# Weights 48 bytes instead of 64 behind the streamed operands, modulo 128, in a two-layer decoder trunk

## The chip, the cores and the metric

The kernel runs on one core of a Trainium2 chip. The metric is the device time of one execution in microseconds (us), the median of several executions.

## The reference

Two layers over 256 tokens of width 1024. Each layer normalizes its input, projects it once into the columns of three token mixers (retention, forgetting attention, RWKV-7) and three gates, merges the mixers' outputs by the gates, projects, and adds a SwiGLU feed-forward block.

```python
for l in range(DEPTH):                       # DEPTH = 2
    h = _rmsnorm(x, mix_norm[l])             # x: (1, 256, 1024)
    proj = (h @ w_in[l]).astype(jnp.float32)
    ret_c, fox_c, rwkv_c, gate_c = jnp.split(proj, splits, axis=-1)
    y_ret = _retention_branch(ret_c, ...)
    y_fox = _fox_branch(fox_c, ...)
    y_rwkv = _rwkv7_branch(rwkv_c, ...)
    gates = jax.nn.sigmoid(gate_c).reshape(B, S, N_BRANCH, D)
    merged = (gates[:, :, 0] * (y_ret @ p_ret[l])
              + gates[:, :, 1] * (y_fox @ p_fox[l])
              + gates[:, :, 2] * (y_rwkv @ p_rwkv[l]))
    x = x + merged @ w_out[l]
    h = _rmsnorm(x, ffn_norm[l])
    g, u = jnp.split(h @ w_gate_up[l], 2, axis=-1)
    x = x + (jax.nn.silu(g) * u) @ w_down[l]
```

Everything is float32.

## The kernel before

**Matrix products in three parts.** Tokens lie along the free axis (256 columns), features on the 128 partitions. Each float32 operand is split into a high part, rounded to the matmul type fp32r, and a low part, the rest. A product of one 128x128 block of weights with 256 tokens is then three matmuls into one accumulator (`mm3`): high weights by high tokens, high weights by low tokens, low weights by high tokens. The weights are the operand that is loaded into the array (LDWEIGHTS, 128 columns), the tokens are streamed past it (MATMUL, 256 columns). Every matmul loads anew, so the PE queue is a strict alternation of loads and matmuls, and a load runs beside the matmul ahead of it. Two groups of products turn the roles round (`gemm_n`, tiles `mqk` and `mv`): the tokens are loaded, and 512, 260 or 256 columns of weights are streamed.

**Where weights come from.** `_piece` takes 1 MB of weights by one DMA into a tile `raw` (three buffers). ACT writes the high part of a piece of up to 1040 columns into `whi`, DVE the low part into `wlo` (pool `spl`, four buffers each), three pieces ahead of their use (`refill`). A piece holds eight 128x128 blocks, so it feeds 24 matmuls.

**Where the streamed tokens lie.** The normalized input is in tiles `xh` and `xl` (pool `xp`), the feed-forward's hidden units in `hi` and `lo` (pool `hp`), the mixers' outputs in `hi` and `lo` of the pool `t2`. A tile's row in a partition is 2048 bytes, two streams of 1024 bytes. Pools lie one behind the other in SBUF, in the order `cp`, `raw`, `spl`, `xp`, and then `big`, `t2`, `sm` for the mixers or `hp`, `ft` for the feed-forward. The allocator puts a tile at a multiple of 32 bytes. Three small tiles that `pad` makes, one at the head of each of `xp`, `big` and `hp`, shift what lies behind them; a buffer of `whi` or `wlo` is 4224 bytes (33 times 128) and one of `raw` 8320 (65 times 128), so all buffers of a pool stand alike modulo 128.

In the built program the streamed tiles of all three pools start at 32 modulo 128, and `whi` and `wlo` at 96. I call the address of the loaded operand less that of the streamed one, modulo 128, their distance. In `mm3` it is 64 throughout (weights less tokens). In `gemm_n` it is tokens less weights: 64 for 512 and 256 columns, and for 260 columns, whose rows are 1040 bytes, it goes 64, 48, 32, 16 over the four blocks of a piece.

The scheduler keeps each engine's instructions in an order that the same code always gives; `PACE` holds the planner's numbers and isn't touched.

Of the kernel before, what the change touches and what calls it, by code (L numbers as in the profile page):

```python
# [9 lines left out]
F32R = mybir.dt.float32r  # L10
# [6 lines left out]
P = 128  # L17
# [143 lines left out]
class Kernel:  # L161
    def __init__(self, ctx, tc, d, depth=DEPTH, debug=None):
        self.tc, self.nc, self.d, self.depth = tc, tc.nc, d, depth
        self.debug = debug or {}
        nc = self.nc
        e = ctx.enter_context
        self.cp = e(tc.tile_pool(name="cp", bufs=1))
        self.raw = e(tc.tile_pool(name="raw", bufs=3))
        self.spl = e(tc.tile_pool(name="spl", bufs=4))
        self.xp = e(tc.tile_pool(name="xp", bufs=4))  # L170
        self.ps = e(tc.tile_pool(name="ps", bufs=4, space=bass.MemoryType.PSUM))
        self.dr = e(tc.tile_pool(name="dr", bufs=1, space=bass.MemoryType.DRAM))
        self.uid, self.pend = 0, None


        zero = self.cp.tile([P, T], mybir.dt.bfloat16, name="zero")
        nc.vector.memset(zero, 0.0)
        pz = self.ps.tile([P, T], F32, tag="sm", bufs=SM, name="pz")
        for _ in range(20):
            self.mmul(pz, zero[:, 0:P], zero, start=True, stop=True)  # L180
        par = [self.cp.tile([P, P_RES], F32, name=f"par{l}") for l in range(depth)]

        self.pad(self.xp, 16)
        self.xt = [self.xtile(f"x0_{j}") for j in range(4)]
        self.jobs, self.raws, self.ready, self.cur = list(self.weights()), [], [], []
        w = [self.raw.tile([P, 2080], F32, tag="raw", name=self.nm("raw")) for _ in range(3)]

        nc.sync.dma_start(w[0][:, 0:1024 + KT], d["x0"])
        self.first = self.halves(w[0][:, 512:1024])
        self.gain = w[0][:, 1024:1024 + KT], self.cp.tile([P, KT], F32, name="gain0")  # L190
        nc.gpsimd.tensor_copy(self.gain[1], self.gain[0])
        nc.sync.dma_start(w[1][:, 0:1536], d["win0"][0, :, 512:2048])
        nc.sync.dma_start(w[2][:, 0:1024], d["win0"][1, :, 0:1024])
        nc.sync.dma_start(self.xt[1], d["xt"][:, 2:4, :])
        nc.sync.dma_start(w[2][:, 1024:2048], d["win0"][1, :, 1024:2048])
        nc.sync.dma_start(self.xt[2], d["xt"][:, 4:6, :])
        self.jobs[0:2] = [(w[0], 2, P, 0), (w[0], 2, P, 2), (w[1], 4, P, 0), (w[1], 8, P, 4), (w[2], 16, P, 0)]
        self.par = par
        self.con = con = self.cp.tile([P, C_RES], F32, name="con")
        self.identb, self.maskb = zero[:, 0:P], zero[:, P:]  # L200
        self.c = {}
        for k, (o, n) in C_OFF.items():
            if k in FETCHED:
                continue
            v = con[:, o:o + n]
            if k in C_SHAPE:
                v = v.rearrange("p (a b) -> p a b", a=C_SHAPE[k][0])
            self.c[k] = v
        cc = self.c["cc"]
        self.cc = lambda i: cc[:, i:i + 1]  # L210
# [87 lines left out]
    def _piece(self):  # L298

        nc = self.nc  # L300
        if not self.raws:
            src, n, width, o = self.jobs.pop(0)
            if hasattr(src, "shape") and src.shape[-1] == n * width:
                raw = self.raw.tile([P, 2080], F32, tag="raw", name=self.nm("raw"))
                nc.sync.dma_start(raw[:, :n * width], src)
            else:
                raw = src
            per = min(8, 1040 // width)
            for s in range(0, n, per):
                self.raws.append((raw, o + s, min(per, n - s), width))  # L310
        raw, s, m, width = self.raws.pop(0)
        r = raw[:, s * width:(s + m) * width]
        hi = self.spl.tile([P, 1056], F32R, tag="whi", name=self.nm("whi"))
        lo = self.spl.tile([P, 1056], F32R, tag="wlo", name=self.nm("wlo"))
        nc.scalar.copy(hi[:, :m * width], r)  # L315
        nc.vector.tensor_tensor(out=lo[:, :m * width], in0=r, in1=hi[:, :m * width].bitcast(F32), op=ALU.subtract)  # L316
        self.ready.append([(hi[:, i * width:(i + 1) * width], lo[:, i * width:(i + 1) * width]) for i in range(m)])
# [1005 lines left out]
```

## Time and profile before

| | |
|---|---|
| median of three runs | 781.5 us (780.92 to 782.41) |
| profiled execution, its own time | 780.94 us |
| its span, first to last instruction | 779.2 us |
| PE busy | 771.7 us, 7000 matmuls |
| DVE busy | 569.0 us |
| ACT busy | 410.6 us |
| granted TensorE clock | 1.00 |

Matmuls overlap in the records, so PE's busy time says only that it never stood still for long. What one matmul costs in the stream is the step from its start to the start of the next, and it is read from start times: a count of instructions in a stretch, divided into the stretch. PEld rows are the weight loads.

### The profile page before, as it was taken

Reading aid. Unit: us, or ns where it says so; the run is one execution under the profiler, and the core shown is the slowest. Engines: PE = TensorE matmul, PEld = TensorE weight load, DVE = VectorE, ACT = ScalarE, POOL = GpSimd, SP = SyncE. Lnnn points to the kernel's source line nnn. Section 1 sums busy time; section 2 is a strip of 40 time slices with the busy share of each in tenths; the row PEclk is TensorE's granted clock in tenths of the full one; section 3 lists DMA queues with packets and bytes.
Section 4 is the critical chain, followed back from the end, with each engine's and each line's share of the span. In section 5 each row is a group of like instructions: output and inputs, shape, how many; then the busy total and the mean of one; then the engine's idle time right before and its main releaser. Section 6 shows DMA issues by size and latency. Waiting matters only on the chain. (4 is left out here: it accounts for less than half of the span.)

```text
span 779.2 us, 16469 instructions
## 1 busy us (share of the span) xinstructions
PE 771.7 (99%) x7000; PEld 754.4 (97%) x7000; DVE 569.0 (73%) x882; ACT 410.6 (53%) x578; POOL 16.7 (2%) x54
## 2 busy tenths in 40 slices
PE   9999999999999999999999999999999999999998
PEld 8899999999999999999998998999999999999998
DVE  7886999688776666655678679987788776666442
ACT  6776555445664445444447855544456554444331
POOL 4000000000000000000020000000000000000000
PEclk9999999999999999999999999999999999999999
DMA  9656445235655555556564453551464556555650
GB/s 340 223 217 188 152 137 206 83 137 216 210 183 188 192 205 180 197 177 209 173 219 169 170 163 126 170 191 62 169 226 173 185 195 214 171 211 171 213 185 28
DMA packets 28235, 140.69 MB, mean 181 GB/s; under 512 B 7648, under 2 KB 9216, under 8 KB 13312
## 3 DMA queue, kind: packets, MB, share of 16 engines
q1 hardware_dynamic: 28160, 139.63, 51.7%
q8 instruction: 55, 0.90, 0.5%
q14 instruction: 20, 0.16, 0.1%
HBM read 137.24 MB, written 1.33 MB: 178 GB/s over the span
## 5 line engine op out<-in xcount | busy, mean ns | idle before, releaser
L315 ACT CAST whi<-raw 128x1024 fp32r<-128x1024 f32 (+3 forms) x258 | 265.1, 1030 | 298.5 <-PE mm L227 215.4
L316 DVE TENSOR_TENSOR wlo<-raw,whi 128x1024 fp32r<-128x1024 f32 (+3 forms) x258 | 308.4, 1199 | 141.1 <-ACT whi L315 140.5
L227 PE MATMUL mm<-xh,whi 128*128 128x256 f32 x1312 | 359.9, 280 | 0.3 <-DVE xh L482 0.2
L227 PE MATMUL mm<-xh,wlo 128*128 128x256 f32 x1312 | 357.7, 279 | 0.0
L227 PE MATMUL mm<-xl,whi 128*128 128x256 f32 x1312 | 357.2, 278 | 0.0
L227 PEld LDWEIGHTS mm<-xh,whi 128*128 128x128 f32 x1312 | 243.5, 188 | 1.1 <-ACT whi L315 0.4
L227 PEld LDWEIGHTS mm<-xh,wlo 128*128 128x128 f32 x1312 | 242.9, 188 | 0.6 <-DVE wlo L316 0.2
L227 PEld LDWEIGHTS mm<-xl,whi 128*128 128x128 f32 x1312 | 243.0, 188 | 0.6 <-DVE xl L491 0.2
L227 PE MATMUL mm<-hi,whi 128*128 128x256 f32 x576 | 160.0, 278 | 0.0
L227 PE MATMUL mm<-hi,wlo 128*128 128x256 f32 x576 | 159.7, 277 | 0.0
L227 PE MATMUL mm<-lo,whi 128*128 128x256 f32 x576 | 159.5, 277 | 0.0
L227 PEld LDWEIGHTS mm<-hi,whi 128*128 128x128 f32 x576 | 108.2, 188 | 0.4
L227 PEld LDWEIGHTS mm<-hi,wlo 128*128 128x128 f32 x576 | 108.2, 188 | 0.3 <-issue 0.3
L227 PEld LDWEIGHTS mm<-lo,whi 128*128 128x128 f32 x576 | 108.1, 188 | 0.1
L699 DVE TENSOR_TENSOR t<-mm,rstd 128x512 f32<-128x512 f32 (+1 forms) x24 | 15.2, 646 | 9.3 <-PE mm L227 8.7
L705 DVE TENSOR_TENSOR h<-t,mm 128x512 f32<-128x512 f32 x22 | 15.1, 687 | 9.4 <-PE mm L227 8.6
L227 PE MATMUL mv<-whi,xh 128*128 128x260 f32 (+1 forms) x64 | 18.7, 292 | 0.0
L227 PE MATMUL mv<-wlo,xh 128*128 128x260 f32 (+1 forms) x64 | 18.2, 285 | 0.0
L648 DVE SCALAR_TENSOR_TENSOR gate<-gate,mm 128x512 f32<-128x512 f32 x24 | 16.1, 679 | 2.8 <-PE mm L227 2.8
L227 PE MATMUL mv<-whi,xl 128*128 128x260 f32 (+1 forms) x64 | 18.1, 283 | 0.0
L640 DVE TENSOR_TENSOR gate<-mm,rstd 128x512 f32<-128x512 f32 x24 | 16.5, 687 | 1.2 <-PE mm L227 0.9
L641 ACT ACTIVATE gate<-gate 128x512 f32<-128x512 f32 x24 | 15.1, 631 | 4.0 <-DVE gate L640 4.0
(252 smaller groups left out, 647.3 us busy)
## 6 DMA issues: line engine op xcount, KB each, us to landing
raw<-in_wg SPq DMA_DIRECT2D x44, 1024.0 KB
raw<-in_wgate SPq DMA_DIRECT2D x24, 1024.0 KB
raw<-in_wd SPq DMA_DIRECT2D x16, 1024.0 KB
raw<-in_win SPq DMA_DIRECT2D x12, 1024.0 KB
raw<-in_wo SPq DMA_DIRECT2D x8, 1024.0 KB
raw<-in_wd SPq DMA_DIRECT2D x8, 768.0 KB
raw<-in_wqk SPq DMA_DIRECT2D x4, 1024.0 KB
raw<-in_pp SPq DMA_DIRECT2D x4, 1024.0 KB
```

The costliest lines, as they stand in the source:

```text
L227: return self.pinned(self.nc.tensor.matmul(*a, **k))
L315: nc.scalar.copy(hi[:, :m * width], r)
L316: nc.vector.tensor_tensor(out=lo[:, :m * width], in0=r, in1=hi[:, :m * width].bitcast(F32), op=ALU.subtract)
L640: nc.vector.tensor_tensor(out=g, in0=ps, in1=self.b2(rstd), op=ALU.mult)
L641: nc.scalar.activation(g, g, AF.Tanh, scale=0.5)
L648: nc.vector.scalar_tensor_tensor(out=g, in0=g, scalar=1.0, in1=ps, op0=ALU.add, op1=ALU.mult)
L699: nc.vector.tensor_tensor(out=t[:, o, :], in0=p, in1=self.bs(rstd, o), op=ALU.mult)
L705: nc.vector.tensor_tensor(out=h, in0=t, in1=pu, op=ALU.mult)
```

## The change

Two edits, no instruction added, removed or moved. The pad tile at the head of `xp` grows from 16 to 20 floats; with the allocator's step of 32 bytes, all that lies behind it moves up by 32 bytes. The tiles `whi` and `wlo` are taken from their fifth element on, 16 bytes further.

```diff
-        self.pad(self.xp, 16)
+        self.pad(self.xp, 20)
...
-        hi = self.spl.tile([P, 1056], F32R, tag="whi", name=self.nm("whi"))
-        lo = self.spl.tile([P, 1056], F32R, tag="wlo", name=self.nm("wlo"))
+        hi = self.spl.tile([P, 1056], F32R, tag="whi", name=self.nm("whi"))[:, 4:]
+        lo = self.spl.tile([P, 1056], F32R, tag="wlo", name=self.nm("wlo"))[:, 4:]
```

| start modulo 128 | before | after |
|---|---|---|
| `whi`, `wlo` | 96 | 112 |
| streamed `xh`, `xl`, `hi`, `lo` | 32 | 64 |
| distance in `mm3` | 64 | 48 |
| distance in `gemm_n`, 512 and 256 columns | 64 | 80 |
| distance in `gemm_n`, 260 columns, block by block | 64, 48, 32, 16 | 80, 64, 48, 32 |
| `con` (identity, masks), `raw` | 32, 96 | 32, 96 |

All other tiles of `xp` and of the pools behind it move by the same 32 bytes and keep their distances to each other. The order of instructions is the same on every engine; one memset of the pad writes four more floats.

## The prediction

> **What bounds the kernel now.** I read the page first, for the engines' shares.
>
> ```profile
> span 779.2 us, 16469 instructions
> PE 771.7 (99%) x7000; PEld 754.4 (97%) x7000; DVE 569.0 (73%) x882; ACT 410.6 (53%) x578; POOL 16.7 (2%) x54
> PEclk9999999999999999999999999999999999999999
> ```
>
> PE is never without work, at full clock. Next the chain of work that ended last, in order of time (start, us, what, count), and what the weight loads waited for (us in total, times, longest):
>
> ```profile
> 555.70 46.26 PE mm L227 x408
> ...
> 602.30 8.53 PE mm L227 x72
> ...
> 611.26 164.60 PE mm L227 x1449
> ...
> PEld mm L227 <- ACT whi L315: 0.4, 1, 0.4
> ...
> PEld mm L227 <- DVE wlo L316: 0.2, 1, 0.2
> ```
>
> The chain is matmuls of line 227 in an unbroken file. Loads waited 0.6 us in all for the split weights, so neither ACT, DVE nor the DMAs set the pace. But the pace isn't uniform: 164.60 / 1449 = 113.6 ns a matmul in one piece, 8.53 / 72 = 118.5 in another of the same instructions. To see why, I asked for stretches, weight loads of line 227 alone (stretch, length, busy and count, clock, DMA share, GB/s); one load of each count reaches over an edge.
>
> ```profile
> 229.03:329.67 100.64, 100.64 (x889) 1.00 0.55 192
> 216.41:223.01 6.60, 6.60 (x57) 1.00 0.42 159
> ...
> 329.67:335.32 5.65, 5.65 (x49) 1.00 0.57 203
> 335.32:389.73 54.41, 54.41 (x482) 1.00 0.56 189
> ```
>
> Two paces: 100.64 / 888 = 113.3 ns, which I call quick, and 6.60 / 56 = 117.9 or 5.65 / 48 = 117.7, which I call slow, at the same clock. There is little between them. Slow stretches begin where the stream was disturbed (small matmuls of the mixers, a new tile) and last some 50 matmuls; quick ones last until the next disturbance. The wide matmuls are these groups, each of them three times over (high by high, high by low, low by high):
>
> ```profile
> L227 PE MATMUL mm<-xh,whi 128*128 128x256 f32 x1312 | 359.9, 280 | 0.3 <-DVE xh L482 0.2
> L227 PE MATMUL mm<-hi,whi 128*128 128x256 f32 x576 | 160.0, 278 | 0.0
> ```
>
> 3 x (1312 + 576) = 5664 of them. Of the 5537 steps from one to the next that the start times give without a break, 4439 are quick (113.3 on average) and 1098 slow (117.9). The slow kind costs 1098 x 4.6 = 5.0 us in all; if all were slow, it would be 4439 x 4.6 = 20.3 us more. These two amounts are the scale of everything below.
>
> **The change, part by part.** The sum is made against the profiled execution, 780.94 us with a span of 779.2; the median of the runs is 781.5, 0.6 above, and I give the forecast against the median.
>
> 1. The pad's memset, 16 to 20 floats on POOL:
>
> ```profile
> L233 POOL MEMSET pad<- x5: 112/113/118, 0.7 to 578.9; 128x16 f32 x3, 128x24 f32 x2
> ```
>
> Forms of 16 and of 24 floats all take 112 to 118 ns, and this one lies at the start, ahead of the first data. Nothing, to within 6 ns.
>
> 2. The splits now write at 16 modulo 32 and read as before. No row has that offset; the nearest is the write of `pj`, whose rows start one float (4 bytes) off the grid, against an aligned write of the same shape:
>
> ```profile
> L640 DVE TENSOR_TENSOR gate<-mm,rstd 128x512 f32<-128x512 f32 x24 | 16.5, 687 | 1.2 <-PE mm L227 0.9
> L747 DVE TENSOR_TENSOR pj<-mm,rstd 128x512 f32<-128x512 f32 x7 | 4.5, 685 | 0.0
> L316 DVE TENSOR_TENSOR wlo<-raw,whi 128x1024 fp32r<-128x1024 f32 x243 | 296.8, 1224 | 134.5 <-ACT whi L315 133.8
> L315 ACT CAST whi<-raw 128x1024 fp32r<-128x1024 f32 x243 | 254.6, 1050 | 285.1 <-PE mm L227 205.7 <-issue 67.7 <-DMA raw<-in_win 4.4
> ```
>
> 685 against 687: no price. The cover, should there be one: a piece feeds 24 matmuls, 24 x 113.3 = 2.7 us, and takes 1.22 us of DVE and 1.05 of ACT; a tenth more on each of 243 pieces is 30 us of a DVE that is idle for 210. Nothing reaches PE.
>
> 3. All tiles behind the pad move by 32 bytes and keep their distances, save against `con`, which stays. That touches the transposes, whose one operand is the identity: for `ptr` from `rav` the distance goes from 32 to 64, from `bk` from 96 to 0. Duration now (ns, min/median/max):
>
> ```profile
> L230 PE MATMUL ptr<-con,rav x16: 272/273/328, 102.7 to 489.0; 128*128 128x128 f32 x16
> ...
> L230 PE MATMUL ptr<-con,bk x16: 272/272/273, 106.9 to 493.3; 128*128 128x128 f32 x16
> ```
>
> The two kinds stand at different distances and take the same. I take nothing; at 1 ns for each of some hundred transposes it is 0.1 us either way.
>
> 4. The distance of the 5664 wide matmuls, 64 to 48: the one term that counts. The trace holds a small trial of it. In `mv` with 260 columns the first block of a piece stands at distance 64 and the second at 48, six matmuls each, in the same stream. Starts of the first block, the second and the third, for the three pieces in which nothing breaks in:
>
> ```profile
> 40.45 0.28 PE L227 MATMUL mv<-whi,xh 128*128 128x260 f32 x1
> ...
> 41.17 0.29 PE L227 MATMUL mv<-whi,xh 128*128 128x260 f32 x1
> ...
> 41.89 0.28 PE L227 MATMUL mv<-whi,xh 128*128 128x260 f32 x1
> ...
> 45.45 0.28 PE L227 MATMUL mv<-whi,xh 128*128 128x260 f32 x1
> ...
> 46.17 0.28 PE L227 MATMUL mv<-whi,xh 128*128 128x260 f32 x1
> ...
> 46.89 0.28 PE L227 MATMUL mv<-whi,xh 128*128 128x260 f32 x1
> ...
> 423.92 0.28 PE L227 MATMUL mv<-whi,xh 128*128 128x260 f32 x1
> ...
> 424.64 0.29 PE L227 MATMUL mv<-whi,xh 128*128 128x260 f32 x1
> ...
> 425.36 0.28 PE L227 MATMUL mv<-whi,xh 128*128 128x260 f32 x1
> ```
>
> At 64: 0.72, 0.72, 0.72 us. At 48: 0.72, 0.72, 0.72. That is 120 ns a matmul both ways, and the second block even streams from an address at 16 modulo 32. The rows resolve 0.01 in 0.72, 1.4% each, about 0.8% over three: 1 ns a matmul, 5.7 us over 5664. So the price is 0, with ends at -5.7 and +5.7 from this trial. What it can't say: 120 is the slow pace (117.9 x 260 / 256 = 119.7); nothing there runs at the quick one, so it is silent on whether the quick pace holds at 48. For that there is only the bound from the stretches, +20.3 if no step stays quick. I take 0, since this is the only row of this very step, and keep -5.7 and the upper end for the range. The reversed matmuls, 512 and 260 columns, go to other distances; at 96 or so of each and 5 ns they can move 1 us at most.
>
> [...]
>
> Sum: 0 + 0 + 0 + 0 on 780.94, so 781.5 at the median.
>
> **The rivals.** *The quick pace is lost, in part or in all (slower).* Load and stream go side by side, and whatever makes 117.9 of 113.3 may need less of a disturbance at 48. For it: addresses do have a say. In 17 places the pace falls from slow to quick inside a run of wide matmuls, at the first block of a new piece; the first and the last of them:
>
> ```profile
> 57.83 0.28 PE L227 MATMUL mm<-xh,whi 128*128 128x256 f32 x1
> ...
> 721.28 0.28 PE L227 MATMUL mm<-hi,whi 128*128 128x256 f32 x1
> ```
>
> In 16 of the 17 that block stands at distance 64 modulo 256, in one at 192, though pieces alternate between the two. After the change these are 48 and 176, and if the way back from slow to quick is gone, slow stretches last. Against it: quick holds for 888 steps through dozens of pieces of both kinds, so it isn't delicate. Price: all slow 801.8; half of the quick ones slow 781.5 + 10.2 = 791.7. It shows from 340 more slow steps on (1.6 us), when the quick share falls from 80% to 74%.
>
> *The slow stretches end sooner or don't arise (faster).* For it: the same 16 of 17. Against it: they begin at disturbances that stay. Price: at most -5.0, and with 512 and 260 columns some -1: 775.5; half of them gone, 779.
>
> *The quick pace itself falls.* Line 230's transposes, each with a load of 128 columns too, follow each other faster:
>
> ```profile
> 106.93 1.04 PE L230 MATMUL ptr<-con,bk 128*128 128x128 f32 x8
> ```
>
> (1.04 - 0.27) / 7 = 110 ns. At 110 the wide ones would save 4439 x 3.3 + 1098 x 7.9 = 23 us: 758. Against it: their streams are half as long, so it needn't be a floor that a distance frees. [...]
>
> That the change doesn't do what it says is ruled out: the built program's addresses stand at 112 and 64. That PE doesn't notice is the forecast.
>
> **How the numbers follow.** No more than 0.2% (1.6 us, about what a measurement of this kernel can tell from no change) either way: 0.36, carried by the equal 0.72 rows. Slow stretches shorter or gone, 775.5 to 779.9: 0.28. The quick pace lower: 0.03. More slow steps, 783.1 to 792: 0.22. Most quick steps lost, 792 to 802: 0.11. The forecast is the likeliest, 781.5. The range 776 to 792 leaves out the third and the last case and the tip of the second, some 0.16. Faster 0.31, same 0.36, slower 0.33. The forecast's own range is 779.9 to 783.1.
>
> **What would show it.** Right: the stretch of gate and up products near 230 to 328 again at 113.3, some 1100 slow steps, the first blocks of `mv` at 0.72. Wrong by the first rival: wide stretches at 117.9 (855 loads in 100.6 us instead of 888), DVE and ACT groups unchanged. Wrong by the second: the piece of 72 after the norm's sum near 602 at 113.3. Casts above 1.05 and 1.22 us would fault step 2, and then loads would wait for `whi` or `wlo`. What would make it wrong above all: that six matmuls at the slow pace say nothing about the quick one.

## The result, and the profile after

The changed kernel takes 809.49 us (809.24 to 809.64), against 781.21 for the kernel before: 1.036 times as long (95% interval 1.035 to 1.038). The profiled execution took 809.64 us. From the page of the changed kernel, the span, PE's row and the granted clock:

```profile
span 807.9 us, 16469 instructions
PE 800.7 (99%) x7000; PEld 783.5 (97%) x7000; DVE 569.7 (71%) x882; ACT 409.4 (51%) x578; POOL 16.7 (2%) x54
PEclk9999999999999999999999999999999999999999
```

The instructions, the clock and the busy time of DVE and ACT are those of before within 0.3%; PE takes longer over the same matmuls, 800.7 us busy against 771.7. Here are the same three pieces of its chain in order of time (start, us, what, count):

```profile
572.24 48.71 PE mm L227 x408
...
621.29 8.61 PE mm L227 x72
...
630.33 174.22 PE mm L227 x1449
```

46.26, 8.53 and 164.60 us have become 48.71, 8.61 and 174.22. The piece of 72, which ran at the slow pace before (118.5 ns), gained 0.08 us; the long one went from 113.6 to 120.2 ns a matmul. So the loss is in what ran at the quick pace. One stretch of the first feed-forward block in both kernels, weight loads of line 227 (stretch, length, busy and count, clock, DMA share, GB/s), before and then after:

```profile
240.00:320.00 80.00, 80.00 (x707) 1.00 0.56 198
```

```profile
240.00:320.00 80.00, 80.00 (x665) 1.00 0.52 185
```

One load of each count reaches over an edge: 80 / 706 = 113.3 ns before, 80 / 664 = 120.5 after. How the new pace is made up shows in the order of time, start by start. At 248.48 a piece of weights begins whose distance is 176 modulo 256 (address of the loaded operand less that of the streamed one), at 251.32 one at 48, at 254.27 one at 176 again; 24 matmuls each.

```profile
248.48 0.28 PE L227 MATMUL mm<-xh,whi 128*128 128x256 f32 x1
...
251.32 0.28 PE L227 MATMUL mm<-xh,whi 128*128 128x256 f32 x1
251.44 0.29 PE L227 MATMUL mm<-xl,whi 128*128 128x256 f32 x1
251.57 0.28 PE L227 MATMUL mm<-xh,wlo 128*128 128x256 f32 x1
251.68 0.29 PE L227 MATMUL mm<-xh,whi 128*128 128x256 f32 x1
251.81 0.28 PE L227 MATMUL mm<-xl,whi 128*128 128x256 f32 x1
...
254.27 0.28 PE L227 MATMUL mm<-xh,whi 128*128 128x256 f32 x1
```

The piece at 176 took 2.84 us, 118.3 ns a matmul; that at 48 took 2.95, 122.9, and in it long and short steps alternate (0.13, 0.11, 0.13: 130 and 117 ns in the records). Not all pieces at 48 are like that: of 88 whole ones 58 go at 123 ns and 30 at 118, so that blocks at 48 average 120.8 and those at 176 118.3. Over the whole run, the 5509 unbroken steps between wide matmuls average 119.5 ns against 114.2 before. 5509 x 5.3 = 29.2 us; the profiled executions differ by 28.7.

What did not change: the splits (DVE and ACT, busy us and mean ns) and the pad's memset, now with a form of 20 floats.

```profile
L316 DVE TENSOR_TENSOR wlo<-raw,whi 128x1024 fp32r<-128x1024 f32 x243 | 296.7, 1224 | 149.9 <-ACT whi L315 149.6
L315 ACT CAST whi<-raw 128x1024 fp32r<-128x1024 f32 x243 | 254.2, 1048 | 315.4 <-PE mm L227 224.9 <-issue 79.8 <-DMA raw<-in_win 4.4
L233 POOL MEMSET pad<- x5: 111/114/119, 0.7 to 596.2; 128x24 f32 x2, 128x16 f32 x2, 128x20 f32 x1
```

### The profile page after: what moved, and what is told of

The parts are those of the page before. It is cut to its first block, busy times and chain, and to the rows that moved or that the text cites. A ratio compares the mean times of both kernels' runs of the same rounds, so it can differ in the third digit from the quotient of the medians.

```text
span 807.9 us, 16469 instructions
## 1 busy us (share of the span) xinstructions
PE 800.7 (99%) x7000; PEld 783.5 (97%) x7000; DVE 569.7 (71%) x882; ACT 409.4 (51%) x578; POOL 16.7 (2%) x54
## 5 line engine op out<-in xcount | busy, mean ns | idle before, releaser
L227 PE MATMUL mm<-xh,whi 128*128 128x256 f32 x1312 | 366.2, 285 | 0.7 <-ACT whi L315 0.5
L227 PE MATMUL mm<-xl,whi 128*128 128x256 f32 x1312 | 363.7, 283 | 0.0
L227 PE MATMUL mm<-xh,wlo 128*128 128x256 f32 x1312 | 363.7, 283 | 0.0
L227 PE MATMUL mm<-hi,whi 128*128 128x256 f32 x576 | 163.2, 283 | 0.0
L227 PE MATMUL mm<-lo,whi 128*128 128x256 f32 x576 | 163.1, 283 | 0.0
L227 PE MATMUL mm<-hi,wlo 128*128 128x256 f32 x576 | 162.6, 282 | 0.0
```

The costliest lines, as they stand in the source:

```text
L227: return self.pinned(self.nc.tensor.matmul(*a, **k))
```

## The experiments

Two theories at the start. Theory D: what counts is the distance between the operand that is loaded and the one that is streamed past. The rivals: it is the place of one operand in itself, the streams' start (A) or the weights' start at 16 modulo 32 (B). All ratios below are against the kernel before, taken with the experiment.

**Both operands moved by 32 bytes, distance 64** (`e1_d64_moved`), **and distance 48 at another place** (`e2_d48_moved`), against the kernel before:

```diff
-        self.pad(self.xp, 16)
+        self.pad(self.xp, 24)      # e2: 32
...                                 # whi and wlo alike
-        hi = self.spl.tile([P, 1056], F32R, tag="whi", ...)
+        hi = self.spl.tile([P, 1056], F32R, tag="whi", ...)[:, 8:]      # e2: 12
```

> Weights and streamed operands both moved by 32 bytes (weights at 0, streams at 64 modulo 128), so the distance is 64 as before. Theory D (the distance between the loaded and the streamed address decides): the pace of before, 113.3 ns with some 118, 781 us within 2. Rival A (where the operands lie in themselves decides, the streams' start at 64 instead of 32 above all): the pace of the changed kernel, 118 to 124 ns, about 809 us.

> Both moved by another 32 bytes against the changed kernel (weights at 16, streams at 96 modulo 128), distance 48 as there. Theory D: the changed kernel again, 809 us within 2, alternating steps of 117 and 130 ns on one half of the pieces. Rival A: something else, since both operands lie elsewhere; about 781 if the streams at 64 were the cause.

Measured: 780.55 us, 0.999 of before (0.998 to 1.000), and 810.45 us, 1.038 (1.036 to 1.039). The stretch of 240 to 320 us in the one and in the other:

```profile
240.00:320.00 80.00, 80.00 (x707) 1.00 0.56 198
```

```profile
240.00:320.00 80.00, 80.00 (x665) 1.00 0.53 185
```

Same distance, same count, at either place of the operands: 707 as before, 665 as after. Rival A falls: the streams of `e1_d64_moved` start where those of the changed kernel do.

**Each half of the change alone**: `e3_weights_only` has the `[:, 4:]` without the pad (distance 80), `e4_streams_only` a pad of 24 without the `[:, 4:]` (the same 32 bytes, distance 32).

> The weights' half of the change alone: weights at 112, streams at 32, distance 80. Theory D: a pace of its own that no run has shown yet, the same on pieces that stand alike modulo 256; between 781 and 810 us by the two distances known. Rival B (weights that start at 16 modulo 32 cost time, in the load or in the splits' writes): 809 us, and every step slower. If it is 781, B falls.

> The pad's half of the change alone: weights at 96, streams at 64, distance 32. Theory D: a pace of its own; if the loss grows on the way from 64 to 48, it goes on: 810 to 830 us. Rival A: 809 us. Rival B: 781 us, since the weights lie where they were.

Measured: 800.31 us, 1.025 (1.023 to 1.026), and 806.56 us, 1.033 (1.031 to 1.034); the same stretch:

```profile
240.00:320.00 80.00, 80.00 (x681) 1.00 0.54 188
```

```profile
240.00:320.00 80.00, 80.00 (x673) 1.00 0.52 185
```

Either half alone loses most of it. Rival B falls with `e4_streams_only`, where the weights lie as before. At 80 the time lies between the two known distances, as theory D allowed. The loss at 32 is less than at 48 and below the 810 us set for it, so it doesn't grow steadily with the way from 64.

**Other distances**: 0 (`e5_d0`: pad 32), 96 (`e6_d96`: `[:, 8:]`), 112 (`e7_d112`: `[:, 12:]`), 68 (`e9_d68`: `[:, 1:]`) and 60 (`e10_d60`: pad 24 and `[:, 7:]`).

> Weights at 96, streams at 96 modulo 128: distance 0, which modulo 256 is 0 on one half of the pieces and 128 on the other. Known so far: mean step 114.2 ns at 64, 119.0 at 32, 119.6 at 48, 117.8 at 80. Theory D with 64 as one good place among several 64 bytes apart (a period of 64): about 114.2 and 781 us. Theory D with a period of 128 or more: a loss like that of 32 or larger, 805 to 820 us.

> Weights at 0, streams at 32 modulo 128: distance 96. Theory D with a loss that falls again beyond 80: 117 ns and 795 us or less. With a period of 64 it should be like 32: 119.0 ns and 806 us. Rival A', that a start at a multiple of 128 or of 64 is good in itself: 781 us.

> Weights at 16, streams at 32 modulo 128: distance 112. With a period of 64 it should be like 48, the changed kernel: 119.6 ns, 809 us, with steps of 130 ns. With a period of 128: unknown, between the value at 96 and that at 0.

> Weights one float further than in the kernel before: distance 68. Known mean steps: 114.2 ns at 64, 117.8 at 80, 119.6 at 48. Theory D with a smooth loss around 64: about a quarter of the way to 80, 115.1 ns and 786 us. Rival: the quick pace is a lock that holds in a band around 64, 781 us; or that holds at 64 alone, 117 to 118 ns and 797 to 802 us.

> Distance 60 (weights at 124, streams at 64). Smooth loss: about a quarter of the way to 48, 115.6 ns and 789 us. A band around 64: 781 us. 64 alone: 117 ns or more, 797 us or more.

All distances measured modulo 128 (each with one half of the pieces 128 further, modulo 256), with the mean of some 5500 steps worked out from each run's start times:

| distance | time, us | ratio to before (95%) | mean step, ns |
|---|---|---|---|
| 0 | 807.42 | 1.034 (1.032 to 1.035) | 119.2 |
| 32 | 806.56 | 1.033 (1.031 to 1.034) | 119.0 |
| 48 (the change) | 809.49 | 1.036 (1.035 to 1.038) | 119.5 |
| 60 | 806.04 | 1.032 (1.031 to 1.034) | 119.0 |
| 64 (before) | 781.21 | 1 | 114.2 |
| 68 | 803.55 | 1.029 (1.027 to 1.031) | 118.2 |
| 80 | 800.31 | 1.025 (1.023 to 1.026) | 117.8 |
| 96 | 797.51 | 1.021 (1.020 to 1.023) | 117.2 |
| 112 | 807.36 | 1.034 (1.032 to 1.035) | 119.1 |

A period of 64 bytes is out (0 isn't like 64, nor 96 like 32), and a start at a multiple of 64 or 128 is no merit in itself (96 has its weights at 0, and takes 797.51 us). And there is no band around 64: one float to either side costs most of the loss, the last of the three cases named for them (at 68 a little more than the 797 to 802 us set for it). The first stretch of 80 us at 68:

```profile
240.00:320.00 80.00, 80.00 (x679) 1.00 0.53 186
```

80 / 678 = 118.0 ns in the very stretch that runs at 113.3 at distance 64. In this kernel half of the blocks stand at 68 modulo 256 and half at 196; of the 2812 unbroken steps at 68 none took 114 ns or less, and of the 2813 at 60 in `e10_d60` ten did.

**Half of the pairs at a wrong distance.** In `e11_lo48` the streams stand 32 bytes further, the high weights too, the low weights only 16.

```diff
+        self.pad(self.xp, 24)
...
+        hi = ...[:, 8:]
+        lo = ...[:, 4:]
```

> High weights at distance 64, low weights at 48. If the loss is made by the pair that runs at the same time (a load beside the matmul ahead of it), only steps with a load of low weights beside them pay, one in three: a third of the changed kernel's loss, 114.2 + 5.3 / 3 = 116.0 ns, 790 us, with the long steps on the matmul of low tokens, beside which low weights are loaded. Rival: one wrong distance breaks the quick pace for all: 805 us or more, every kind of step longer.

Measured: 796.08 us, 1.019 (1.018 to 1.021), mean step 117.0 ns. Neither: more than a third of the loss (5.3 / 3 = 1.8 ns, measured 2.8), less than all of it. Steps beside a load of low weights average 117.0, those beside a load of high weights 116.5 and 117.5, though the load stands at 64 from the stream that it runs beside. The longest are not those that I had named, but those of the matmul whose own weights are the low ones. So in this run a pair at 48 took the quick pace from its neighbours at 64 as well (114.2 before).

**What is slowed, the load or the stream?** `e12_half_stream` is the kernel before, `e13_half48` the changed kernel, each with half streams in two of three matmuls (which leaves out the low parts for half of the tokens):

```diff
-        self.mmul(out, wh, xl, start=False, stop=False)
-        self.mmul(out, wl, xh, start=False, stop=last)
+        self.mmul(out[:, 0:P], wh, xl[:, 0:P], start=False, stop=False)
+        self.mmul(out[:, 0:P], wl, xh[:, 0:P], start=False, stop=last)
```

> The kernel before, but the second and third matmul of each product stream 128 of the 256 tokens, so the low parts are left out for the other half. What sets the quick step of 113.3 ns: if the load of 128 columns does, steps beside a full load stay near 113 with half the stream, and the time stays within 10 us of 781. If the stream of 256 columns does, two of three steps shorten, to the 110 ns of the transposes or lower, and the time falls by 3760 x 3.3 = 12 us or more.

> The changed kernel (distance 48), but the second and third matmul of each product stream 128 of the 256 tokens, so the low parts are left out for the other half. At distance 64 and full clock such steps took 113.3 ns (353 loads in 40 us). If a wrong distance slows the stream, which then ends after the load, half streams hide it: 113.3 ns and 353 loads in 40 us of full clock, or nearly so. If it slows the load, the steps stay near the changed kernel's 119.6 ns: 335 in 40 us. [...]

Each ran once, and both executions are longer than 781 us, 901.08 and 842.08, in the main because the clock fell in some stretches (last section); my 10 us for the first were wrong. Span times mean granted clock, 899.1 x 0.887 and 840.2 x 0.957, gives an estimate of 798 and 804 us at full clock. At full clock the steps can be read. Weight loads of line 227 in the feed-forward's first products, in the first at 64:

```profile
320.00:360.00 40.00, 40.00 (x353) 1.00 0.56 200
360.00:400.00 40.00, 40.00 (x353) 1.00 0.53 185
```

and in the second at 48, with the changed kernel's own row for the same kind of products behind it:

```profile
240.00:280.00 40.00, 39.95 (x353) 1.00 0.55 188
320.00:360.00 40.00, 40.00 (x355) 1.00 0.54 187
```

```profile
240.00:280.00 40.00, 40.00 (x334) 1.00 0.53 185
```

353 to 355 loads in 40 us is 113.0 to 113.6 ns a load, at either distance; with whole streams at 48 it was 334, 120 ns. The loads keep this time on average; the matmuls now start unevenly, 0.17, 0.06 and 0.11 us apart, as four starts of `e12_half_stream` show:

```profile
330.18 0.33 PE L227 MATMUL mm<-xh,whi 128*128 128x256 f32 x1
330.35 0.22 PE L227 MATMUL mm<-xl,whi 128*128 128x128 f32 x1
330.41 0.28 PE L227 MATMUL mm<-xh,wlo 128*128 128x128 f32 x1
330.52 0.33 PE L227 MATMUL mm<-xh,whi 128*128 128x256 f32 x1
```

Two things follow. With less to stream the loads came no closer together than 113.0 to 113.6 ns, so at the quick pace the step isn't set by the length of the stream; that it is set by the load of 128 columns is my reading (a load of another width wasn't tried). And distance 48 doesn't lengthen the load by itself: the 6.8 ns that it costs with whole streams (113.3 to 120.1) are gone when two of three streams are short. If a load were slowed for as long as a stream runs beside it, two thirds of the streamed columns would leave two thirds of the loss of 6.8 ns, an estimated 117.8 ns or some 340 loads in 40 us, and that isn't what came. My reading of these counts is that at 48 the stream of 256 columns takes longer, and not the load. No run here shows that: in the profile the ends of matmuls are modelled.

**64 or 192 modulo 256.** Before, half of the wide matmuls stand at 64 modulo 256 and half at 192. `e8_all64` and its repetition `e15_all64_again` put all at 64, `e14_all192` all at 192; buffers of 4352 bytes stand alike modulo 256.

```diff
-        hi = self.spl.tile([P, 1056], F32R, tag="whi", ...)
+        hi = self.spl.tile([P, 1088], F32R, tag="whi", ...)[:, 32:]     # e14: without the slice
...
-            self.pad(hp, 16)
+            self.pad(hp, 48)
```

> The weights' buffers are 4352 bytes (17 times 256) instead of 4224, and the hidden units' pool is moved by 128, so that every wide matmul stands at distance 64 modulo 256, where before half stood at 64 and half at 192. In the kernel before, the pace fell from slow to quick on blocks at distance 64 in 16 of 17 places. Theory D256 (the period is 256, and 64 is the better half): slow stretches end at once, fewer than 500 slow steps, 776 to 779.5 us. Rival D128 (the period is 128, the 16 of 17 is something else): 781 us within 1.6.

> Buffers of 4352 bytes as in the run with all matmuls at 64 modulo 256, but at 192. If 64 is the better half (770 slow steps and 779.6 us there): more slow steps than the 1098 of the kernel before, 782 to 785 us. If the two halves are alike: 781 us within 1, and the 16 of 17 places were no sign of a distance.

> The version with all wide matmuls at distance 64 modulo 256 once more, beside the kernel before in more rounds: faster by 0.1 to 0.2% again (779.6 to 780.3 us) if the shorter slow stretches are real; within 0.05% if not.

Measured: 779.64 us, 0.998 (0.9975 to 0.9994); 799.34 us, 1.023 (1.021 to 1.025); 779.67 us, 0.998 (0.9970 to 0.9988). The 80 us stretch at 192 and at 64 (the repetition):

```profile
240.00:320.00 80.00, 80.00 (x680) 1.00 0.53 189
```

```profile
240.00:320.00 80.00, 80.00 (x708) 1.00 0.57 198
```

At 192 alone the quick pace is all but gone (200 quick steps against 5336 slow), far beyond the 782 to 785 that I had set. At 64 alone there are 770 and, in the repetition, 600 slow steps, where the kernel before has 1098; I had set fewer than 500, so slow stretches shrink there but don't end at once. A period of 128 bytes is out, and 256 fits: 64 and 320 modulo 512, which these kernels hold about half and half, average 113.98 and 113.94 ns in `e8_all64`. Of the eighteen residues modulo 256 that ran, 64 is the one at which 113.3 ns is seen both to begin and to hold; only 64 and 192 ran alone, the others in pairs 128 apart. So I put the quick steps of blocks at 192 in the kernel before down to the blocks at 64 that lie between them: alone they ran at 799.34 us, among blocks at 64 at 781.21. The version with all blocks at 64 is faster than the kernel before by 0.2%, and the fastest that ran.

## Why the prediction was wrong

It forecast 781.5 us with a range of 776 to 792; the time was 809.49.

- Steps 1 to 3 were right: the memset takes 111 to 119 ns, the splits 1224 and 1048 ns, and the transposes `ptr` the median of 273 and 272 that they had.
- Step 4 failed: the term "distance of the wide matmuls, 64 to 48" was put at 0, and it is some +29 (29.2 by the steps, 28.7 between the profiled executions). The 0 came from six matmuls of 260 columns per piece. Those rows were right, and they are right after the change, where the first block stands at 80 and the second at 64:

```profile
41.11 0.29 PE L227 MATMUL mv<-whi,xh 128*128 128x260 f32 x1
...
41.83 0.28 PE L227 MATMUL mv<-whi,xh 128*128 128x260 f32 x1
...
42.55 0.28 PE L227 MATMUL mv<-whi,xh 128*128 128x260 f32 x1
```

  0.72 and 0.72 again, while the wide matmuls lost 5.3 ns each. Rows that take 0.72 us, 120 ns a matmul, at each distance that they pass can't show what a distance does to a pace of 113.3. The prediction said that the rows were silent on the quick pace, and still took their 0 for it.
- The upper end was wrong too. "All slow", 801.8, took 117.9 for the worst pace. At distance 48 two of three pieces go at 123 ns with steps of 130, a pace that no stretch of before shows. The sign named for this rival, 855 loads in the stretch of 100.64 us, came as 836.
- The first rival, the quick pace lost, is what came: a mean step of 119.5 ns where it was 114.2. It had 0.11 for most quick steps lost, and the reason against it was the step that misled: quick held "for 888 steps through dozens of pieces of both kinds, so it isn't delicate". `e14_all192` speaks for what that was: with all blocks at 192 only 200 steps were quick, so the blocks at 64 seem to have carried those at 192. At one float from 64 it is gone: at 68 none of 2812 steps took 114 ns or less.
- The sign that the prediction read for its rivals, 16 of 17 places at 64 modulo 256, was good: 64 is where the quick pace begins, and with all blocks there slow stretches shrink as the second rival had it, for 1.4 to 1.6 us of its 5.
- The third rival, a quick pace below 113.3, came at no distance that ran, and with half streams, at 64 and 48, 353 to 355 loads in 40 us is that pace again.
- Two readings of the prediction were loose and changed nothing: slow stretches last from some 5 to 62 matmuls, not some 50 throughout, and 855 loads belong to steps of 117.7 ns (at 117.9 it would be 853).
- The same loads and streams took 113.3 or 120.5 ns in the stretch of 240 to 320 us by their distance alone, 64 or 48. By what mechanism, no run here shows.

## What to carry to other kernels

In this kernel, where each matmul has a load of 128 columns and they follow each other without a gap, the distance in bytes between the loaded and the streamed operand was a parameter of its own, worth 2 to 4% (797.51 to 810.45 us away from 64 and 192, 781.21 before). Where a kernel has such a stream of matmuls, measure the distance in steps as fine as the data type allows, and modulo 256, not 128. Judge it by the step from start to start in an undisturbed stretch: PE's busy share was 99% before and after, and the waits named no cause (0.6 us of loads waiting for split weights before, 0.9 after). A pace that was quick through two kinds of blocks, 113.3 ns, didn't hold for one of them alone, 80 / 679 = 117.8 ns at 192, and the rows of 260 columns, 0.72 us for six at 64, 48 and 80 alike, didn't settle it for those of 256.

## What the runs showed of the hardware, unexpected

The good place is narrow: at 60 and 68, one float to either side of 64, the kernel loses 3.2 and 2.9%, like distances far off.

With half streams the granted clock fell to one half in stretches of both kernels (mean 0.887 and 0.957), where with whole streams it was 1.00 on average. It began to fall where PE also stood still for a part of the time: in `e12_half_stream` PE was busy for 35.36 of the 40 us from 40 on (clock 0.91) and for 3.50 of the 5 us from 175 on, just ahead of the long fall. That the one brings the other about, no run here shows: it then stayed at one half although loads and matmuls followed without a gap. Weight loads of line 227 in `e12_half_stream`:

```profile
240.00:280.00 40.00, 40.00 (x189) 0.50 0.33 112
```

and in `e13_half48`, during its fall and behind it:

```profile
185.00:190.00 5.00, 5.00 (x25) 0.50 0.00 0
200.00:205.00 5.00, 5.00 (x46) 1.00 0.11 44
```

Behind this fall the clock was full again only after 300 us in the first kernel and by 200 us in the second. What makes the difference between the two stays open. At half clock the loads came 40 / 188 = 213 ns apart, less than twice 113.3. By these two steps, if loads set the pace at both clocks, an estimated 2 x 113.3 - 213 = 14 ns of the quick step don't grow when the clock is halved.
